# When the parts of a transposed chunk are made: moved delays in the feed-forward rounds of a two-layer decoder trunk

## The chip, the cores and the metric

The kernel runs on one core of a Trainium2 chip. The metric is the device time of one execution in microseconds (us); lower is better. Before the change the median of three runs is 2461.22 us (2460.16 to 2461.9).

## What is computed

Two decoder layers act on x, 256 positions by 2048 features in float32. Cut to what matters here:

```
for l in range(2):
    h = rms_norm(x, mix_norm[l])
    q, k, v, uv, gate_logits = split(h @ w_in[l])
    branch_a = sliding_window_attention(rope(norm(q)), rope(norm(k)), v, sinks[l]) @ w_attn_branch[l]
    branch_b = chunked_sgu(gelu(uv), w_spatial[l], b_spatial[l], ...) @ w_sgu_branch[l]
    g = sigmoid(gate_logits)
    x = x + (g[:2048] * branch_a + g[2048:] * branch_b) @ w_out[l]
    h2 = rms_norm(x, ffn_norm[l])
    x = x + (silu(h2 @ w_gate[l]) * (h2 @ w_up[l])) @ w_down[l]      # 5632 hidden features
```

In `chunked_sgu` each group of 128 features is mixed over positions by the lower triangle of a 128 by 128 matrix of `w_spatial`; the kernel needs these matrices transposed.

## The kernel before, in words

**Products.** All weights pass once through the core, in tiles of 256 rows by 512 columns (`raw`, 512 KB each). A float32 product is made of three products of parts: ScalarE rounds a weight tile to its high part (`whi`, L244), VectorE subtracts to get the low part (`wlo`, L245), and TensorE (PE) does high by high, low by high and high by low (L340, L341). The other operand, the activations, is held transposed and split in the same way: `uh` and `ul`. A list `entries`, written out before the kernel's first instruction, holds the order of all weight tiles. `step` (L343) handles one entry: it asks for weight loads up to 7 entries ahead on SyncE's queue (SP), for parts up to 4 entries ahead, and issues the entry's matmuls: twelve (both halves of 128 positions) for most entries, six for the entries of the next paragraph.

**Fewer products.** Where two products share an operand (gate and up, or two column chunks), one or two blocks of 512 rows are done with seven products of sub-blocks in place of eight, the way of Winograd. These entries are P1 to P7. P5, P6 and P7 need sums of activations, `sums`, with their own parts `sh` and `sl`, and four of the entries need differences of weight tiles (`raw<-raw,raw`, L229, on VectorE). Between P5 and P6 ScalarE takes the product in PSUM away (`kept`, L363) and copies one bank into the other (L364); P6 adds to a bank that L364 reads.

**Ticks.** `tick` (L265) comes after every twelve matmuls. `after(n, fn)` puts work on the list for the n-th tick from now. The instructions of such work stand on VectorE behind the newest weight-part instruction that has been issued there, so about three entries ahead of PE. PE's own order is as written; on the other engines the order comes from a scheduler that goes by the order of issue and by what it expects to be ready.

**Feed-forward.** The 11 chunks of 512 hidden features are done in ROUNDS of 4, 4 and 3 chunks (f0 to f1). For every chunk `hidden` (L976) makes gate and up, puts silu(gate) times up into `hid` (L981, L985) and calls `transposed` (L421). After the chunks of a round follow the products with `w_down` for these rows (`hid` plans), whose first head entries (P1, P5, P6, P2, P7, P4) are placed between the last entries of the last chunk. In rounds 1 and 2 the first three chunks use two blocks of the P kind each (`two`).

**Transposing a chunk.** `turn` (L403) transposes 32 by 32 blocks on VectorE (`box`, L410), half at the call and half one tick later, and then issues 16 DMAs of 32 KB (`tt<-box`, L416) that gather the blocks: all on the given queue, or with `queue=None` alternately on SP's and on GpSimd's (POOL). For most chunks the parts `uh`, `ul` are made 6 and 7 ticks after the call (`parts`, L435 on ScalarE and L436 on VectorE), shifted by `late`. Chunk 0 of a round, the Winograd one, runs down six steps at the ticks of a tuple such as WINO_HID: two of `scaled` (L480, ScalarE: `flat<-tt`), `whole` (L484 `uh`, L485 `ul`), two of `sums` (L499, two VectorE instructions each), and `finished` (L484 `sh`, L485 `sl`). Chunk 2 of the last round goes through PE transposes instead (L453).

In `hidden` before, the call comes 2 ticks after the chunk (1 for the fourth chunk, 3 for the last chunk of the last round), the queue is POOL's, except for the fourth chunk, which uses both.

**Spatial matrices.** `fetch_large` (L663) loads the matrices 21 and 25 ticks after a layer's start (SP, with the triangle cut on POOL, L615) and at tick 40 calls `spatial` (L648): PE turns eight of them into two PSUM buffers `pw` (L653), VectorE copies each out (L654 `wsT<-pw`). These buffers come from a pool of two, `ps_tr`, which the attention's transposed weights `ppt` (L783) use as well.

Of the kernel before, what the change touches and what calls it, by code (L numbers as in the profile page):

```python
# [33 lines left out]
WINO = 0  # L34
# [1 line left out]
WINO_IN = 6, 7, 8, 12, 13, 14  # L36
WINO_FIRST = 6, 7, 8, 9, 10, 11
WINO_MIX = 6, 7, 9, 10, 11, 13
WINO_HID = 7, 8, 17, 18, 19, 20
W_SPLIT = 4  # L40
W_TWO = 24
W_SUM = 6
# [16 lines left out]
def hybrid_trunk(ctx: ExitStack, tc: tile.TileContext, x, mix_norm, w_in, q_norm, k_norm, sinks,  # L59
                 sgu_ln_g, sgu_ln_b, w_spatial, b_spatial, w_attn_branch, w_sgu_branch, w_out,  # L60
                 ffn_norm, w_gate, w_up, w_down, cosine, sine, out):
    nc = tc.nc
# [19 lines left out]
    def slot(shape, dt=F32, name="s"):  # L82
        return big.tile(shape, dt, tag="s4", name=nm(name))
# [178 lines left out]
    def after(n, fn):  # L262
        steps.append((slot_no[0] + n, fn))

    def tick():  # L265
        slot_no[0] += 1
        due = [s for s in steps if s[0] <= slot_no[0]]
        steps[:] = [s for s in steps if s[0] > slot_no[0]]
        for _, fn in sorted(due, key=lambda s: s[0]):
            with tc.issue_after(stream.last.ins):  # L270
                fn()
# [116 lines left out]
    def product(key):  # L388

        p = run(key)  # L390
        while p.left:
            step()
        return p.acc["a"]

    def product_pair(key, on_a, on_b):


        p = run(key)
        p.calls = (on_a, on_b)
        while p.left:  # L400
            step()
# [179 lines left out]
    def mix_cols(l):  # L581
        return vcols[:, l * 16:(l + 1) * 16]

    def ffn_cols(l):
        return vcols[:, NB + l * 16:NB + (l + 1) * 16]
# [72 lines left out]
    def prepare(l):  # L658
        layer[l] = pl = Layer(l)
        after(5, lambda: pl.tables(0))  # L660
        after(6, lambda: pl.tables(1))

    def fetch_large(pl):  # L663
        for n, i in ((13, 2), (17, 3), (21, 0), (25, 1)):
            after(n, lambda i=i: pl.fetch(i))
        after(40, pl.spatial)

    class Attention:

# [210 lines left out]
    def residual(key, nxt=None, scale=1.0, store=False):  # L880

        def chunk(j, sums):
            for t in range(NT):
                n = 2 if store and j == NCH - 1 else 1
                w = CW // n
                for i in range(n):
                    sl = slice(j * CW + i * w, j * CW + (i + 1) * w)
                    nc.vector.scalar_tensor_tensor(out=xs[:, t, sl], in0=sums[t][:, i * w:(i + 1) * w], scalar=scale,  # L888
                                                   in1=xs[:, t, sl], op0=ALU.mult, op1=ALU.add)
                    if store:  # L890
                        eng = nc.sync if i == 0 else nc.scalar
                        eng.dma_start(out[0, t * P:(t + 1) * P, sl], xs[:, t, sl])
            if nxt is not None:
                last = j == NCH - 1 and not nxt.soon
                after(1 if last else 2, lambda: nxt.unit(j, j > 0 and nxt.soon, queue=None if last or j == WINO and not nxt.soon else nc.gpsimd,
                                                         late=-2 if last else 0))
                after(3, lambda: nxt.squares(j))
                if j == NCH - 1:
                    after(4, lambda: nxt.finish())
                    if not nxt.soon:  # L900
                        after(W_TWO, lambda: nxt.unit(WINO + 1, again=True))

        for j in range(0, NCH, 2):
            product_pair(key, lambda sums: chunk(j, sums), lambda sums: chunk(j + 1, sums))
        return nxt
# [4 lines left out]
    for l in range(DEPTH):  # L910

        gates = {}
        att, spa = Attention(layer[l]), Spatial(layer[l], norm)
        units_at["att", l], units_at["sgu", l] = att.attT, spa.sguT
        fetch_large(layer[l])

        def taken(kind, c):

            def by(ps):
                if kind in ("v", "u"):  # L920
                    (spa.v if kind == "v" else spa.u)(c, ps)
                    return
                dst = slot([P, NT, CW], name=kind)
                for t in range(NT):
                    nc.scalar.activation(dst[:, t, :], ps[t], AF.Tanh if kind == "gate" else AF.Copy,
                                         scale=(norm.rh if kind == "gate" else norm.r)[t])
                if kind == "gate":
                    gates[c] = dst
                else:
                    att.keys(dst) if kind == "kv" else att.queries(c, dst)  # L930
            return by

        def projected(*chunks):
            if len(chunks) == 2:
                product_pair(("in", l), taken(*chunks[0]), taken(*chunks[1]))
            else:
                taken(*chunks[0])(product(("in", l)))
                tick()

        for chunks in FIRST_PART[l]:  # L940
            projected(*chunks)


        for j in range(NCH):
            ps = product(("att", l))
            ga = gates[j]
            for t in range(NT):
                nc.vector.scalar_tensor_tensor(out=ga[:, t, :], in0=ga[:, t, :], scalar=1.0, in1=ps[t],
                                               op0=ALU.add, op1=ALU.mult)
            tick()  # L950
        mT = units_at["mix", l] = [None] * NCH
        nxt = Norm(ffn_cols(l))
        units_at["ffn", l] = nxt.units
        for j in range(NCH):
            if j == 1:
                projected(("gate", 5), ("gate", 6))
            if j == 3:
                projected(("gate", 7))
            ps = product(("sgu", l))
            ga, gb = gates[j], gates[NCH + j]  # L960
            for t in range(NT):
                nc.vector.scalar_tensor_tensor(out=gb[:, t, :], in0=gb[:, t, :], scalar=1.0, in1=ps[t],
                                               op0=ALU.add, op1=ALU.mult)
                nc.vector.tensor_tensor(out=ga[:, t, :], in0=ga[:, t, :], in1=gb[:, t, :], op=ALU.add)
            after(2 + 2 * (j == NCH - 1), lambda j=j, ga=ga: transposed(mT, j, ga, on_pe=j == NCH - 1,
                                                                   wino=WINO_MIX if j == WINO else None,
                                                                   late=3 if j == NCH - 2 else 0))
            tick()

        norm = residual(("mix", l), nxt, scale=0.5)  # L970


        if l + 1 < DEPTH:
            after(28, lambda: prepare(l + 1))

        def hidden(hT, c):  # L976
            hid = slot([P, NT, CW], name="hid")

            def on_gate(g):
                for t in range(NT):  # L980
                    nc.scalar.activation(hid[:, t, :], g[t], AF.Silu, scale=norm.r[t])  # L981

            def on_up(up):
                for t in range(NT):
                    nc.vector.scalar_tensor_tensor(out=hid[:, t, :], in0=up[t], scalar=norm.r[t], in1=hid[:, t, :],  # L985
                                                   op0=ALU.mult, op1=ALU.mult)
                pe, soon = c == len(hT) - 1 == 2, c == 3
                after(3 if pe else 1 if soon else 2,
                      lambda: transposed(hT, c, hid, on_pe=pe, wino=WINO_HID if c == WINO else None,
                                         queue=None if soon else nc.gpsimd, late=-2 if soon else 0))  # L990

            product_pair(("ffn", l), on_gate, on_up)

        for r, (f0, f1) in enumerate(ROUNDS):
            hT = units_at["hid", l, r] = [None] * (f1 - f0)
            for f in range(f0, f1):
                hidden(hT, f - f0)
            if f1 < NF:
                residual(("hid", l, r))
            elif l + 1 < DEPTH:  # L1000
                norm = Norm(mix_cols(l + 1), True)
                units_at["in", l + 1] = norm.units
                residual(("hid", l, r), norm)
            else:
                residual(("hid", l, r), store=True)
# [37 lines left out]
```

## Time and profile before

| | |
|---|---|
| median of three runs | 2461.22 us |
| the profiled execution | 2457.45 us |
| its span, first to last instruction | 2455.7 us |
| PE busy | 2438.1 us, 99% |
| VectorE (DVE) busy | 1999.5 us, 81% |
| ScalarE (ACT) busy | 1472.5 us, 60% |
| GpSimd (POOL) busy | 315.6 us, 13% |
| mean granted TensorE clock | 0.999 |

The profile names engines PE, DVE, ACT, POOL and SP; PEld is PE's weight load, SPq the queue of SyncE. A row such as `wlo<-raw,whi` names what is written and read; L245 is the line of the kernel. In the timeline the first number of a row is its start in us from the span's start, the second its length, `x2` means that two such instructions are merged, and `[1.58 <-DVE sl L485]` says that the engine stood idle for 1.58 us before it until that instruction ended. Matmuls overlap: one that takes 0.39 us in its row lets the next start earlier, so starts are compared with starts. In the waits the columns are the total in us, the times, and the longest.

### The profile page before, as it was taken

Reading aid. Unit: us, or ns where it says so; the run is one execution under the profiler, and the core shown is the slowest. Engines: PE = TensorE matmul, PEld = TensorE weight load, DVE = VectorE, ACT = ScalarE, POOL = GpSimd, SP = SyncE. Lnnn points to the kernel's source line nnn. Section 1 sums busy time; section 2 is a strip of 40 time slices with the busy share of each in tenths; the row PEclk is TensorE's granted clock in tenths of the full one; section 3 lists DMA queues with packets and bytes.
Section 4 is the critical chain, followed back from the end, with each engine's and each line's share of the span. In section 5 each row is a group of like instructions: output and inputs, shape, how many; then the busy total and the mean of one; then the engine's idle time right before and its main releaser. Section 6 shows DMA issues by size and latency. Waiting matters only on the chain.

```text
span 2455.7 us, 31363 instructions
## 1 busy us (share of the span) xinstructions
PE 2438.1 (99%) x10968; PEld 2012.6 (82%) x10968; DVE 1999.5 (81%) x2320; ACT 1472.5 (60%) x1842; POOL 315.6 (13%) x592
## 2 busy tenths in 40 slices
PE   9999999999999999999999999999999999999999
PEld 7888888888888888887887888888888888888877
DVE  6798676797978997899877986768878789978996
ACT  5567544576655665566655665545666556655664
POOL 3100002132210111001101000021322101110110
PEclk9999999999999999999999999999999999999999
DMA  9555657576667657665747446675767675667654
GB/s 299 196 187 163 212 198 220 186 236 210 220 217 233 210 176 231 230 203 170 229 155 257 152 157 223 202 215 177 246 202 236 204 245 189 200 209 241 203 179 139
DMA packets 280782, 506.74 MB, mean 206 GB/s; under 512 B 28272, under 2 KB 40144, under 8 KB 280624
## 3 DMA queue, kind: packets, MB, share of 16 engines
q1 hardware_dynamic: 262544, 486.35, 61.0%
q0 software_dynamic: 17760, 18.12, 2.8%
q8 instruction: 86, 1.41, 0.2%
q14 instruction: 72, 0.59, 0.1%
q10 hardware_dynamic: 320, 0.27, 0.0%
HBM read 475.27 MB, written 2.10 MB: 194 GB/s over the span
## 4 chain that ended last, share of the span: by engine, by line
PE 90%; DVE 3%; DMA 3%; SPq 1%; issue 1%; ACT 1%; DVEq 0%; ACTq 0%
PE acc L340 59%; PE acc L341 29%; DMA raw<-in_w_in_dram 2%; DVE wlo L245 2%; SPq L416 1%; ACT whi L244 1%; PE po L793 1%; PE psc L754 0%; PE ppt L783 0%; DVE raw L229 0%; PE psg L871 0%; PE pt L453 0%; DMA raw<-in_w_up_dram 0%; DMA raw<-in_w_down_dram 0%; DVE box L410 0%
## 5 line engine op out<-in xcount | busy, mean ns | idle before, releaser
L244 ACT ACTIVATE whi<-raw 128x1024 fp32r<-128x1024 f32 (+1 forms) x1074 | 1132.0, 1059 | 883.0 <-PE acc L341 623.4
L245 DVE TENSOR_TENSOR wlo<-raw,whi 128x1024 fp32r<-128x1024 f32 (+1 forms) x1075 | 1301.3, 1219 | 399.0 <-ACT whi L244 386.7
L340 PE MATMUL acc<-whi,uh 128*128 128x512 f32 x2994 | 1170.3, 391 | 1.2 <-ACT uh L439 1.2
L340 PE MATMUL acc<-wlo,uh 128*128 128x512 f32 x2994 | 1167.1, 390 | 3.0 <-DVE wlo L245 2.9
L341 PE MATMUL acc<-whi,ul 128*128 128x512 f32 x2994 | 1166.4, 390 | 0.0
L340 PEld LDWEIGHTS acc<-wlo,uh 128*128 128x128 f32 x2994 | 562.6, 188 | 123.2 <-DVE wlo L245 6.0
L340 PEld LDWEIGHTS acc<-whi,uh 128*128 128x128 f32 x2994 | 562.6, 188 | 117.7 <-ACT uh L439 1.4
L341 PEld LDWEIGHTS acc<-whi,ul 128*128 128x128 f32 x2994 | 562.3, 188 | 117.8 <-DVE ul L444 0.5
L416 POOL DMA_DIRECT2D tt<-box x544 | 266.5, 497 | 1697.0 <-ACT whi L244 695.5
L229 DVE TENSOR_TENSOR raw<-raw,raw 128x1024 f32<-128x1024 f32 x236 | 287.8, 1219 | 1.6 <-DMA raw<-in_w_up_dram 0.8
L341 PE MATMUL acc<-whi,sl 128*128 128x512 f32 x472 | 184.0, 390 | 3.2 <-DVE sl L485 3.2
L340 PE MATMUL acc<-whi,sh 128*128 128x512 f32 x472 | 184.8, 392 | 1.7 <-ACT acc L364 1.7
L340 PE MATMUL acc<-wlo,sh 128*128 128x512 f32 x472 | 184.2, 390 | 0.0
L341 PEld LDWEIGHTS acc<-whi,sl 128*128 128x128 f32 x472 | 88.6, 188 | 22.5 <-DVE sl L485 4.0
L340 PEld LDWEIGHTS acc<-whi,sh 128*128 128x128 f32 x472 | 88.6, 188 | 20.9 <-ACT acc L364 2.1
L340 PEld LDWEIGHTS acc<-wlo,sh 128*128 128x128 f32 x472 | 88.7, 188 | 18.0
L366 DVE TENSOR_TENSOR kept<-acc,kept 128x512 f32<-128x512 f32 x94 | 64.3, 684 | 10.1 <-PE acc L341 10.1
L369 ACT ACTIVATE acc<-kept 128x512 f32<-128x512 f32 x94 | 54.9, 586 | 4.3 <-DVE kept L366 4.2
L888 DVE SCALAR_TENSOR_TENSOR xs<-acc,xs 128x512 f32<-128x512 f32 (+1 forms) x66 | 42.0, 668 | 8.4 <-PE acc L341 8.1
L436 DVE TENSOR_TENSOR ul<-tt,uh 128x512 fp32r<-128x512 f32 x52 | 34.0, 684 | 2.9 <-ACT uh L435 2.9
L435 ACT ACTIVATE uh<-tt 128x512 fp32r<-128x512 f32 x52 | 29.8, 618 | 9.4 <-DMA tt<-box 9.4
L312 POOL TENSOR_TENSOR rv<-ve,neg_half 128x4 f32<-128x4 f32 x8 | 11.9, 1486 | 172.9 <-DVE ve L839 159.5
(137 smaller groups left out, 874.8 us busy)
## 6 DMA issues: line engine op xcount, KB each, us to landing
raw<-in_w_in_dram SPq DMA_DIRECT2D x239, 512.0 KB, 4.7
raw<-in_w_gate_dram SPq DMA_DIRECT2D x176, 512.0 KB, 4.4
raw<-in_w_up_dram SPq DMA_DIRECT2D x176, 512.0 KB, 4.9
raw<-in_w_down_dram SPq DMA_DIRECT2D x176, 512.0 KB, 5.0
raw<-in_w_out_dram SPq DMA_DIRECT2D x64, 512.0 KB, 5.0
tt<-box POOLq DMA_DIRECT2D x544, 32.0 KB, 4.2
raw<-in_w_attn_branch_dram SPq DMA_DIRECT2D x32, 512.0 KB, 5.6
raw<-in_w_sgu_branch_dram SPq DMA_DIRECT2D x32, 512.0 KB, 4.4
```

The source lines that it names most:

```text
L229: self.last = nc.vector.tensor_tensor(out=self.raws[d], in0=self.raws[x], in1=self.raws[y], op=ALU.subtract)
L244: self.high = nc.scalar.activation(hi[:, i, :], raw[:, i, :], AF.Copy)
L245: self.last = nc.vector.tensor_tensor(out=lo[:, i, :], in0=raw[:, i, :], in1=hi[:, i, :].bitcast(F32), op=ALU.subtract)
L340: nc.tensor.matmul(ps, a, part[:, kk, :], start=first and kk + n == 0, stop=False, skip_group_check=True)
L341: nc.tensor.matmul(ps, b, hi[:, kk, :], start=False, stop=kk == 1, skip_group_check=True)
L366: nc.vector.tensor_tensor(out=p.kept[:, int(tag == "P7"), :], in0=a[1], in1=p.kept[:, 1, :], op=ALU.add)
L369: nc.scalar.activation(ps, p.kept[:, t, :], AF.Copy)
L416: q.dma_start(dst[j * B:(j + 1) * B, i], box[i * B:(i + 1) * B, j])
L435: nc.scalar.activation(h, s_, AF.Copy)
L436: nc.vector.tensor_tensor(out=l, in0=s_, in1=h.bitcast(F32), op=ALU.subtract)
L793: nc.tensor.matmul(po[:, h, :], pT[kb][:, h, :], self.kv[:, kb, KVW + g * HD:KVW + (g + 1) * HD], start=kb == 0, stop=kb == t)
L888: nc.vector.scalar_tensor_tensor(out=xs[:, t, sl], in0=sums[t][:, i * w:(i + 1) * w], scalar=scale, in1=xs[:, t, sl], op0=ALU.mult, op1=AL ...
```

## The change

It moves work to other ticks and one gather to other queues; no instruction that computes is added or taken away.

```diff
-WINO_HID = 7, 8, 17, 18, 19, 20
+WINO_HID = 11, 12, 17, 18, 19, 20
+WINO_END = 9, 10, 12, 13, 14, 15
...
         for n, i in ((13, 2), (17, 3), (21, 0), (25, 1)):
             after(n, lambda i=i: pl.fetch(i))
-        after(40, pl.spatial)
+        after(34, pl.spatial)
...
-                pe, soon = c == len(hT) - 1 == 2, c == 3
+                pe, soon = c == len(hT) - 1 == 2, c == 3 or c == 1 and len(hT) == 3
                 after(3 if pe else 1 if soon else 2,
-                      lambda: transposed(hT, c, hid, on_pe=pe, wino=WINO_HID if c == WINO else None,
-                                         queue=None if soon else nc.gpsimd, late=-2 if soon else 0))
+                      lambda: transposed(hT, c, hid, on_pe=pe, wino=None if c != WINO else WINO_HID if len(hT) == 4 else WINO_END,
+                                         queue=None if soon else nc.gpsimd, late=-2 if c == 3 else 4 if c == 1 and len(hT) == 4 else 2 if c == 2 else 0))
```

In words, for both layers:

- In the last round (3 chunks) chunk 0 makes `scaled` 2 ticks later, and `whole`, `sums` and `finished` 5 ticks sooner.
- In the last round chunk 1 is transposed 1 tick sooner, its 16 gathers go 8 to SP and 8 to POOL, and its parts come 1 tick sooner.
- In the rounds of 4 chunks, `scaled` of chunk 0 comes 4 ticks later, the parts of chunk 1 come 4 ticks later, and those of chunk 2 come 2 ticks later.
- The spatial matrices are turned at tick 34 of a layer, not 40.

## The prediction

> **What bounds the kernel now.** I read the page first, then the waits of PE, then the timeline around each wait.
>
> ```profile
> span 2455.7 us, 31363 instructions
> PE 2438.1 (99%) x10968; PEld 2012.6 (82%) x10968; DVE 1999.5 (81%) x2320; ACT 1472.5 (60%) x1842; POOL 315.6 (13%) x592
> ...
> PE acc L341 <- DVE sl L485: 3.2, 2, 1.6
> PE acc L340 <- DVE wlo L245: 2.9, 5, 0.8
> PE ppt L783 <- DVE wsT L654: 2.4, 1, 2.4
> PE acc L340 <- ACT acc L364: 1.7, 1, 1.7
> ```
>
> PE bounds it, and nearly all of its time is work that the change leaves alone: 2455.7 − 2438.1 leaves 17.6 us of idle time, the first and last moments included. The four waits named are 10.2 us of that. A change that only moves other engines' work can win those waits and what hangs on them, some 10 us or 0.4%, and no more. So each wait is looked at by itself.
>
> The pitch of a full matmul is needed throughout:
>
> ```profile
> 2359.83 0.39 PE L340 MATMUL acc<-wlo,uh 128*128 128x512 f32 x1
> ...
> 2362.55 0.39 PE L340 MATMUL acc<-wlo,uh 128*128 128x512 f32 x1
> ```
>
> Twelve matmuls, one tick, lie between these two: 2.72 us, 0.227 each.
>
> **Part 1: the last round's first sums.** In the second layer:
>
> ```profile
> 2374.34 0.39 PE L341 MATMUL acc<-whi,ul 128*128 128x512 f32 x1
> ...
> 2377.03 0.50 PE L341 MATMUL acc<-whi,sl 128*128 128x512 f32 x1 [1.58 <-DVE sl L485]
> 2377.37 0.39 PE L340 MATMUL acc<-whi,sh 128*128 128x512 f32 x1
> ```
> ```profile
> 2370.21 0.42 DVE L499 TENSOR_TENSOR sums<-flat 128x256 f32<-128x256 f32 x1
> ...
> 2375.76 1.22 DVE L485 TENSOR_TENSOR sl<-sums,sh 128x1024 fp32r<-128x1024 f32 x1
> ```
>
> The reader sees PE at P5 waiting for `sl`, which VectorE ends at 2376.98. From 2374.34 to 2377.37 four pitches (0.91) took 3.03 us: 2.12 lost. The waits say twice, so each layer has it. WINO_END moves `finished` from 20 to 15: 5 × 2.72 = 13.6 us sooner, so `sl` would start about 2362.2, and even some us late it is there before PE asks at 2375.06. The gather that feeds it ends much earlier than `scaled`, which itself goes two ticks later. I take the whole: **−4.2** for both layers (bounds: 0 if the queues carry it late all the same, −4.2).
>
> **Part 2: the second chunk.** After P5, the second layer alone shows another gap:
>
> ```profile
> 2383.29 0.39 PE L341 MATMUL acc<-whi,ul 128*128 128x512 f32 x1
> ...
> 2385.69 0.40 PE L340 MATMUL acc<-wlo,sh 128*128 128x512 f32 x1
> ```
> ```profile
> 2381.04 1.06 ACT L244 ACTIVATE whi<-raw 128x1024 fp32r<-128x1024 f32 x1 [1.67 <-PE acc L341]
> 2382.01 1.13 ACT L435 ACTIVATE uh<-tt 128x512 fp32r<-128x512 f32 x2
> ...
> 2384.73 0.58 ACT L364 ACTIVATE acc<-acc 128x512 f32<-128x512 f32 x1
> ```
>
> Two pitches (0.45) took 2.40: 1.95 lost. P6 waits for L364 (the waits' last row), which stands in ScalarE's queue behind L435, the second chunk's parts, and behind a `whi` that itself waits for PE. P5's product was complete long before: its sixth matmul starts three pitches after 2377.03. One tick sooner (2.7 us), the parts go ahead of this, and `sh` (1.06) leaves the stretch as well. I take **−1.95**; bounds 0 and −1.95. The gather itself is 16 issues in two batches of 3.91 us on POOL; half of them go to SP, past weight loads:
>
> ```profile
> 716.91 6.07 SPq L416 DMA_DIRECT2D tt<-box  x8
> ...
> 1326.13 10.66 SPq L416 DMA_DIRECT2D tt<-box  x16
> ```
>
> The first row is the fourth chunk of round 0, which already uses both queues: SP is held for 6 us, and no PE wait stands near. In the last round ScalarE's `whi` waits for PE, as the row at 2381.04 says, and not for its load, so I cost the hold at 0; the price without that cover is the second rival's.
>
> **Part 3: VectorE where the sums land.** Here the change pays. Around 2350 VectorE has no gap:
>
> ```profile
> 2350.00:2363.00 13.00, 13.00 (x59) 10.75 (x58) 13.00 (x15) 7.26 (x9) 0.00 (x0) 1.00 0.78 259
> ...
> 2358.72 1.22 DVE L245 TENSOR_TENSOR wlo<-raw,whi 128x1024 fp32r<-128x1024 f32 x1
> 2359.85 0.70 DVE L410 STREAM_TRANSPOSE box<-hid 128x512 f32<-128x512 f32 x1
> 2360.48 2.32 DVE L245 TENSOR_TENSOR wlo<-raw,whi 128x1024 fp32r<-128x1024 f32 x2
> ```
>
> In the first row the third busy time, VectorE's, is 13.00 of 13.00. The `wlo` of 2358.72 ends at 2359.94 and PE reads it at 2362.55 (above): 2.61 us of slack. By the ticks `whole`, four `sums` and one `box` are now issued ahead of it. Queued, an instruction holds VectorE about 0.08 less than its row's length (0.70 for `box`, but the next starts 0.63 later), so they are 1.14 (`ul`, as long as `sl`) + 4 × 0.34 + 0.62 = 3.12 us. The `wlo` is 0.51 late. The next one, from 2360.48, also has `sl` and the second `box` ahead: 1.76 more; it ends about 2365.9, its PE time moves from 2365.27, one tick after 2362.55, to 2365.78: 0.14 late. Each pause costs its first matmul 0.1 (2377.03 to 2377.37 is 0.34). Together 0.85. In the first layer the slack is smaller:
>
> ```profile
> 1137.11 1.22 DVE L245 TENSOR_TENSOR wlo<-raw,whi 128x1024 fp32r<-128x1024 f32 x1
> ...
> 1140.71 0.39 PE L340 MATMUL acc<-wlo,uh 128*128 128x512 f32 x1
> ```
>
> 1140.71 − 1138.33 = 2.38, so 0.23 more: 1.1. I take **+2.0**, from the order of issue and these slacks. Bounds: 0, if the scheduler lets the urgent `wlo` pass; +9.8, if all the moved work, 2 × 1.14 + 4 × 0.34 + 2 × 0.62 = 4.9 us a layer, meets no slack at all. Nothing else new waits on VectorE; ScalarE, with 7.26 busy of 13.00 in that row, has room for `uh` and `sh`.
>
> **Part 4: spatial matrices.**
>
> ```profile
> 1340.91 1.03 PE L653 MATMUL pw<-ident,wsraw 128*128 128x128 f32 x8
> 1341.88 0.72 PE L754 MATMUL psc<-kT,qT 64*128 64x128 f32 x8
> 1345.03 0.66 PE L783 MATMUL ppt<-ident,pr 128*128 128x128 f32 x4 [2.43 <-DVE wsT L654]
> 1345.44 0.48 PE L340 MATMUL acc<-whi,uh 128*128 128x512 f32 x1
> ...
> 1349.40 0.40 PE L340 MATMUL acc<-wlo,uh 128*128 128x512 f32 x1
> ```
> ```profile
> 1341.80 2.57 DVE L245 TENSOR_TENSOR wlo<-raw,whi 128x1024 fp32r<-128x1024 f32 x2 [5.75 <-ACT whi L244]
> 1344.29 1.28 DVE L654 COPY wsT<-pw 128x512 f32<-128x512 f32 x2
> ...
> 1346.10:1349.10 3.00, 3.00 (x9) 2.33 (x8) 3.00 (x5) 1.26 (x3) 0.00 (x0) 0.50 0.69 247
> ```
>
> In the second layer, tick 40 is also a tick of attention. `pw` takes both `ps_tr` buffers, the copies stand behind two late `wlo`, and `ppt` waits for a buffer. Six ticks earlier are 72 matmuls (16.3 us), one set of scores (0.65) and the pause below (1.1): about 1322.8, where PE has a hole:
>
> ```profile
> 1322.58 0.47 PE L340 MATMUL acc<-whi,uh 128*128 128x512 f32 x1
> ...
> 1324.15 0.40 PE L341 MATMUL acc<-whi,ul 128*128 128x512 f32 x1
> ```
>
> Two pitches took 1.57, so 1.1 idle; the eight transposes (0.97, by the next start) fit in. There the copies (1.28) fall behind parts issued three entries ahead of PE, and well before the 5.75 us in which VectorE idles. At the old place only `psc` (0.7) and `ppt` (0.41) stay: PE is at its product at 1342.0, but the first `wlo` ends at 1343.0, so the second matmul starts there, which is like a start at 1342.8. 1345.44 − 1342.8 = 2.6 won. Next late is then the load behind SP's 10.66 us gather, which is that 1343.0.
>
> There is more. After the gap matmuls run at half speed: the last row's clock column says 0.50, and the ten steps from 1345.44 to 1349.40 took 3.96 in place of 2.27, 1.7 lost. With 0.2 for the pause left, the second layer wins 4.1. [...]
>
> The first layer:
>
> ```profile
> 122.95 0.50 PE L340 MATMUL acc<-wlo,uh 128*128 128x512 f32 x1 [0.57 <-DVE wlo L245]
> ...
> 125.58 1.03 PE L653 MATMUL pw<-ident,wsraw 128*128 128x128 f32 x8
> ```
>
> Here `pw` comes after a pause of 0.57 for a late weight, and the first matmul then costs 0.1 more. With 0.97 us of transposes done before it, PE arrives later and the pause goes: −0.7. The copies then stand on VectorE near 110 us, behind parts made ahead of PE, and are waited for by nobody before the mixing. Together **−4.8**. Bounds: −0.7, if in the second layer the copies or the weights hold PE as long as now; −5.0, if the pause left there goes too.
>
> **Part 5: the rounds of four.** In round 1 the second chunk's parts (L436) go through VectorE shortly before a low part is late:
>
> ```profile
> 919.43 0.39 PE L341 MATMUL acc<-whi,ul 128*128 128x512 f32 x1
> 919.88 0.50 PE L340 MATMUL acc<-wlo,uh 128*128 128x512 f32 x1
> ```
>
> 0.45 − 0.23 = 0.2 lost; four ticks later (10.9 us) the parts are past it. For both layers **−0.4**. The other moves there meet no wait of PE: 0, bounds −0.2 and +0.4 by the same row.
>
> **The sum.** −4.2 − 1.95 + 2.0 − 4.8 − 0.4 = −9.4 us (−11.4 without the toll of part 3). Against the profiled execution, 2457.45 (the span and 1.75 around it), that is 2448.1. The median of the runs is 3.8 above the profiled execution; I carry the difference over: 2461.2 − 9.4 = **2451.8 us**. A measurement of this kernel can tell about 0.2%, 4.9 us, from no change.
>
> **Rivals.**
> 1. *VectorE's toll is larger.* If all 4.9 us lie ahead of the `wlo` read at 2362.55 and its like, the toll is 4.9 − 2.61 + 4.9 − 2.38 + 0.2 = 5.0, and the time 2454.8; with no slack, 9.8, and 2459.6. For: no idle time in 13 us. Against: the slacks, and parts issued in turn. Chance 0.16.
> 2. *SP's half of the gather holds up weight loads; slower.* Place: SP's queue in the last round, where the gather first waits for the second `box`. A hold of 10.66 us cost PE at most 0.7 by the rows at 1326 and 1342; a longer one costs one for one. From a hold of 10.66 − 0.7 + 9.4/2 = 14.7 us in each layer on, the kernel is slower. Eight issues take 6; the other 9 would be spent waiting for a `box` late by that much. With 17.2 us per layer: 2466.3. Against: fully busy VectorE was late by about 3 us in part 3. Chance 0.07.
> 3. *The half clock is not in every run.* If the timed runs of before mostly miss it, 1.7 of part 4 isn't there to win: 2453.5. [...] Against: the profiled execution has it and is no slower than the timed ones. [...] Chance 0.12.
> 4. *It doesn't do what it says in the last round.* The order off PE is the scheduler's; L364 was late in one layer and not in the other with the same ticks. If parts 1 and 2 stay as they are and part 3 costs nothing: −5.2, 2456.0. Chance 0.15.
>
> My forecast keeps 0.5, with a range of its own of 2449.5 to 2454 (no toll, or twice the toll). The range for 8 in 10 reaches over rivals 1, 3 and 4: 2449.5 to 2459.5. Faster by over 0.2% means below 2456.3: the forecast, rival 3, and half or more of 1 and 4, 0.78. Same 0.15, slower 0.07.
>
> **What would show it.** Right: no PE wait for `sl`, `wsT` or L364; a `pw` at about 1322 with no 0.50 clock near 1346; one short wait of PE for `wlo` in each last round, near 1141 and 2363. Wrong: `sl` still ending within 2 us of P5; PE waits over 2 us for `wlo` there; ScalarE waiting for `raw` of `w_down`; or a new wait where nothing was moved.

## The result, and the profile after

| | before | after |
|---|---|---|
| median of five runs each | 2460.76 us (2460.16 to 2461.9) | 2449.74 us (2449.56 to 2451.44) |
| the profiled execution | 2457.45 us | 2449.56 us |
| its span | 2455.7 us | 2447.8 us |

The change is faster: ratio 0.9957, 95% interval 0.9942 to 0.9971. The forecast was 2451.8 us in a range of 2449.5 to 2459.5. The timed runs moved by 11.0 us, the profiled executions by only 7.9; where the other 3.1 may come from is taken up below. The change adds a line above the rest, so L340 of before is L341 of after, L364 is L365, and so on.

From the page of after:

```profile
span 2447.8 us, 31373 instructions
...
PE 2436.2 (100%) x10968; PEld 2012.2 (82%) x10968; DVE 1999.0 (82%) x2320; ACT 1470.0 (60%) x1842; POOL 310.6 (13%) x576
```

The waits of PE in after (total, times, longest):

```profile
PE acc L341 <- DVE wlo L246: 2.8, 7, 0.6
PE acc L341 <- DVE kept L367: 1.4, 2, 1.0
PE acc L341 <- ACT uh L440: 1.3, 1, 1.3
PE pwarm L292 <- DVE warm L287: 1.1, 1, 1.1
```

The three waits that the forecast set out to win (`sl`, `wsT`, the copy of one bank into the other) are gone from the list, 7.3 us in all. Those for `wlo` are about as large as before, and one for `kept` (L367) now stands second.

Where P5 gave way to P6 in the second layer, PE's timeline in after shows no gap of two microseconds any more:

```profile
2371.01 0.39 PE L342 MATMUL acc<-whi,sl 128*128 128x512 f32 x1
...
2377.13 0.39 PE L342 MATMUL acc<-whi,ul 128*128 128x512 f32 x1
2377.39 0.50 PE L341 MATMUL acc<-whi,sh 128*128 128x512 f32 x1
```

VectorE's and ScalarE's timelines say why. `sl` ends at 2365.26, 5.7 us before PE reads it, and the second chunk's parts leave ScalarE before the copy (L365), which ends at 2377.33, just when P6 asks:

```profile
2364.03 1.23 DVE L486 TENSOR_TENSOR sl<-sums,sh 128x1024 fp32r<-128x1024 f32 x1
```
```profile
2373.13 1.14 ACT L436 ACTIVATE uh<-tt 128x512 fp32r<-128x512 f32 x2
...
2376.73 0.60 ACT L365 ACTIVATE acc<-acc 128x512 f32<-128x512 f32 x1
```

At the spatial place `pw` stands where it was expected, and `ppt` follows `psc` without a wait:

```profile
1321.24 1.03 PE L654 MATMUL pw<-ident,wsraw 128*128 128x128 f32 x8
...
1340.09 0.66 PE L784 MATMUL ppt<-ident,pr 128*128 128x128 f32 x4
1340.50 0.48 PE L341 MATMUL acc<-whi,uh 128*128 128x512 f32 x1
1340.82 0.39 PE L341 MATMUL acc<-wlo,uh 128*128 128x512 f32 x1
```
```profile
1340.05 2.57 DVE L246 TENSOR_TENSOR wlo<-raw,whi 128x1024 fp32r<-128x1024 f32 x2 [4.63 <-ACT whi L245]
```

The last row, from VectorE's timeline, is the pair of `wlo` that stood at 1341.80 in before. Its first half takes over 1.2 us, so it is not done when PE's matmul on `wlo` starts at 1340.82: PE does not wait for this pair there.

New in after are two pauses of PE 25 to 30 us further on, and two smaller ones like them in the first layer, at 156.78 and 159.11:

```profile
1366.80 0.50 PE L341 MATMUL acc<-wlo,uh 128*128 128x512 f32 x1 [0.51 <-DVE wlo L246]
1370.55 0.50 PE L341 MATMUL acc<-wlo,sh 128*128 128x512 f32 x1 [0.95 <-DVE kept L367]
```

PE's order is the same in both kernels, so the traces can be laid over each other, product matmul by product matmul, and each change of the difference between the two starts put down to its place:

| term | forecast | trace of after less that of before |
|---|---|---|
| 1, first sums | −4.2 | −2.13 and −2.13, +0.17 at P6 behind the first |
| 2, second chunk | −1.95 | −1.81 |
| 3, toll on VectorE in the last rounds | +2.0 | +0.22 in layer 1; +0.69 (at 2331 to 2340) and +0.22 (at 2356) in layer 2 |
| 4, spatial matrices | −4.8 | −0.35 in layer 1; −5.2 in layer 2, 1.59 of it the half clock |
| new pauses in attention | none | +1.3 in layer 1, +1.9 in layer 2 |
| 5, rounds of four | −0.4 | −0.39 and −0.39 |
| all product matmuls, first to last | −9.4 | −8.1 |

The rows leave out shifts of 0.2 us and less elsewhere. One execution of each kernel is compared, and executions differ: in e2 to e6 below, where the first layer's matrices stay at tick 40, the place of row 4 in layer 1 shows −0.35 to −0.46 as well, so this −0.35 is not shown to come from the move. In the other kernels that move them (e1, e7 to e12) it is −0.80 to −1.22, which makes the move worth some 0.4 to 0.8 us there and nothing in the execution of after.

Two questions remain: what gave some 3.2 us back in attention, and whether the parts do alone what they do together.

### The profile page after: what moved, and what is told of

It reads as the page before. It is cut to its first block, busy times and chain, and to the rows that moved or that the text cites. A ratio compares the mean times of both kernels' runs of the same rounds, so it can differ in the third digit from the quotient of the medians.

```text
span 2447.8 us, 31373 instructions
## 1 busy us (share of the span) xinstructions
PE 2436.2 (100%) x10968; PEld 2012.2 (82%) x10968; DVE 1999.0 (82%) x2320; ACT 1470.0 (60%) x1842; POOL 310.6 (13%) x576
## 4 chain that ended last, share of the span: by engine, by line
PE 93%; DVE 3%; DMA 1%; issue 1%; ACT 1%; SPq 0%; POOL 0%; DVEq 0%; ACTq 0%; POOLq 0%
PE acc L341 61%; PE acc L342 30%; DVE wlo L246 1%; DMA raw<-in_w_in_dram 1%; PE po L794 1%; DVE raw L230 0%; SPq L417 0%; PE psc L755 0%; PE ppt L784 0%; PE pt L454 0%; ACT whi L245 0%; PE psg L872 0%; DMA raw<-in_w_up_dram 0%; DVE pr L759 0%; DVE mx L763 0%
## 5 line engine op out<-in xcount | busy, mean ns | idle before, releaser
L341 PE MATMUL acc<-whi,uh 128*128 128x512 f32 x2994 | 1171.3, 391 | 1.3 <-ACT uh L440 1.3
L341 PE MATMUL acc<-wlo,uh 128*128 128x512 f32 x2994 | 1168.2, 390 | 2.8 <-DVE wlo L246 2.8
L341 PEld LDWEIGHTS acc<-wlo,uh 128*128 128x128 f32 x2994 | 562.5, 188 | 123.3 <-DVE wlo L246 7.9
L341 PEld LDWEIGHTS acc<-whi,uh 128*128 128x128 f32 x2994 | 562.5, 188 | 117.4 <-ACT uh L440 1.5
L417 POOL DMA_DIRECT2D tt<-box x528 | 258.6, 497 | 1698.4 <-ACT whi L245 568.1
L341 PE MATMUL acc<-wlo,sh 128*128 128x512 f32 x472 | 184.6, 391 | 1.4 <-DVE kept L367 1.4
L341 PE MATMUL acc<-whi,sh 128*128 128x512 f32 x472 | 185.0, 392 | 0.0
L341 PEld LDWEIGHTS acc<-wlo,sh 128*128 128x128 f32 x472 | 88.7, 188 | 20.1 <-DVE kept L367 2.2
L341 PEld LDWEIGHTS acc<-whi,sh 128*128 128x128 f32 x472 | 88.7, 188 | 18.6 <-ACT acc L365 0.6
L367 DVE TENSOR_TENSOR kept<-acc,kept 128x512 f32<-128x512 f32 x94 | 64.4, 685 | 8.7 <-PE acc L342 8.7
```

The source lines that it names most:

```text
L341: nc.tensor.matmul(ps, a, part[:, kk, :], start=first and kk + n == 0, stop=False, skip_group_check=True)
L367: nc.vector.tensor_tensor(out=p.kept[:, int(tag == "P7"), :], in0=a[1], in1=p.kept[:, 1, :], op=ALU.add)
L417: q.dma_start(dst[j * B:(j + 1) * B, i], box[i * B:(i + 1) * B, j])
```

## The experiments

Theory: each edit removes the wait that the forecast names, the edits add up, and what is given back is VectorE's load. The rivals are written into each expectation. Differences "by place" are found as in the table above, against before. Ratios are to before, measured beside each kernel.

### The parts alone

**e1: the spatial matrices alone.** Before, with

```diff
-        after(40, pl.spatial)
+        after(34, pl.spatial)
```

> Part 4 alone: the spatial matrices at tick 34, all else as before. Theory G (given back): the wait for wsT at 1345 and the half clock after it go (5.2 us in the profile of the changed kernel), but VectorE then has no lead in the attention stretch that follows, and new pauses of PE near 156-160 (1.3 us) and 1366-1371 (1.8 us) come with it; profiled span 2.4 us shorter, by 1.5 to 3.5. Theory I (independent): the new pauses belong to other parts of the change, or to chance in the scheduler's order; then the span is 4.5 to 5.5 us shorter. In both, no wait for wsT and no 0.5 clock near 1346.

Measured: 2455.61 us, ratio 0.9986 (0.9977 to 0.9995), span 2453.4. By place the wins are those of after (layer 2: +0.80, −1.02, −3.38 and −1.59), and the pauses come too: +1.45 in all at 156 to 159, +2.46 at 1369 to 1373. PE's timeline of e1:

```profile
1369.23 0.50 PE L340 MATMUL acc<-wlo,uh 128*128 128x512 f32 x1 [1.12 <-DVE wlo L245]
...
1372.98 0.50 PE L340 MATMUL acc<-wlo,sh 128*128 128x512 f32 x1 [0.95 <-DVE kept L366]
```

So the pauses belong to this edit and to no other: Theory G.

**e2: everything but the spatial matrices.** After, with

```diff
-        after(34, pl.spatial)
+        after(40, pl.spatial)
```

> The change without part 4. Theory G: no pauses of PE over 0.5 us near 156-160 and 1366-1371; the wait for wsT near 1345 and the half clock are back; profiled span 5.5 us shorter than before (2 x 2.1 + 1.8 + 0.8 - 1.1). Theory I: the pauses are there all the same, and the span is 2.5 us shorter. For the timed runs: if the difference between 11.0 (timed) and 7.9 us (profiled) is a matter of half clock windows that the wsT wait brings, the timed gain here stays near 5.5; if it is something else, it is near 8.

Measured: 2452.9 us, ratio 0.9972 (0.9962 to 0.9982), span 2452.1. No such pause in attention; the wait for `wsT` is back (3.0 us), and the mean granted clock is 0.998, against 1.000 in after. The span is only 3.6 us shorter than before's, not 5.5: by place its matmuls near the start lie some 2.5 us behind. The timed gain, 6.6, lies between the 5.5 and the 8 of the expectation and decides nothing. In medians e1 gives −3.8 and e2 −6.6, in sum −10.4, against −11.0 for after: these two halves add up.

**e3: the sums alone.** Before, with WINO_END for chunk 0 of the last round and nothing else:

```diff
-wino=WINO_HID if c == WINO else None,
+wino=None if c != WINO else WINO_HID if len(hT) == 4 else WINO_END,
```

Here WINO_HID keeps its old values.

> Part 1 alone: WINO_END for chunk 0 of the last round. Forecast by the prediction: PE's wait for sl goes in both layers (-4.2), the toll on VectorE comes (+0.2 in the first layer, +0.9 in the second, as the changed kernel's profile has it, against 2.0 on record), and the wait for L364 stays in the second layer (1.8 to 1.95): span 3.1 us shorter. Rival: the toll comes from chunk 1's earlier blocks and not from the sums; then no pause for wlo and 4.2 us shorter.

Measured: 2464.17 us, ratio 1.0019 (1.0011 to 1.0028), span 2461.9: slower than before, where 3.1 us less was expected. The wait for `sl` goes in both layers, −2.13 each. But ScalarE's timeline in the first layer reads:

```profile
1158.62 1.06 ACT L245 ACTIVATE whi<-raw 128x1024 fp32r<-128x1024 f32 x1 [1.54 <-issue]
1161.34 1.06 ACT L245 ACTIVATE whi<-raw 128x1024 fp32r<-128x1024 f32 x1 [1.66 <-PE acc L342]
1162.30 1.13 ACT L436 ACTIVATE uh<-tt 128x512 fp32r<-128x512 f32 x2
1163.34 0.57 ACT L364 ACTIVATE kept<-acc 128x512 f32<-128x512 f32 x1
1163.95 0.58 ACT L365 ACTIVATE acc<-acc 128x512 f32<-128x512 f32 x1
```

and PE's:

```profile
1164.58 0.50 PE L341 MATMUL acc<-whi,sh 128*128 128x512 f32 x1 [3.33 <-ACT acc L365]
```

The sums on VectorE push the second chunk's `box` back. The first POOL gather starts at 1145.82, against 1142.45 in before; PE itself is 1.2 to 1.6 later there, so about 2 us later for PE. PE, on the other hand, comes 2.1 us sooner. The copy that P6 needs stands on ScalarE behind the parts, and these behind a `whi` that waits for PE. P6 is 3.79 and 1.75 late by place, and each time matmuls at half clock follow, 0.43 us apart in place of 0.23 (1.45 and 1.52 us lost by place).

**e4: the second chunk alone.** Before, with

```diff
-                pe, soon = c == len(hT) - 1 == 2, c == 3
+                pe, soon = c == len(hT) - 1 == 2, c == 3 or c == 1 and len(hT) == 3
...
-queue=None if soon else nc.gpsimd, late=-2 if soon else 0))
+queue=None if soon else nc.gpsimd, late=-2 if c == 3 else 0))
```

> Part 2 alone: chunk 1 of the last round one tick sooner, gathered on both queues. By the prediction the wait for L364 goes (-1.9) and the waits for sl stay (3.2 us in all): span 1.9 us shorter. Rival: L364 is late because of sh and the first sums in ScalarE's queue, which part 1 moves; then the wait for L364 stays and the span is within 0.5 us of before.

Measured: 2457.47 us, ratio 0.9993 (0.9984 to 1.0001), span 2456.9. By place the copy's wait goes in layer 2, −1.89; `sl` is waited for as before. In medians e3 and e4 come to +4.7 − 2.0 = +2.7, though e4's interval reaches 1. Together, in e2, which has the rounds of four besides (0 to 0.8 us, e5), they give −6.6. So they do not add: 8 to 9 us hang on their being done at once.

**e5: the rounds of four alone.** Before, with

```diff
-wino=WINO_HID if c == WINO else None,
+wino=None if c != WINO else WINO_HID if len(hT) == 4 else WINO_OLD,
...
-late=-2 if soon else 0))
+late=-2 if c == 3 else 4 if c == 1 and len(hT) == 4 else 2 if c == 2 else 0))
```

Here WINO_HID is 11, 12, 17 to 20 as in after, and WINO_OLD the tuple of before.

> The two edits of the rounds of four chunks alone (the WINO_HID sums four ticks later, the second and third chunks' parts later), the last rounds and the spatial matrices as before. Theory of the prediction: 0.4 us less (0.2 per layer); the trace of after, laid over that of before, showed 0.46 and 0.38, so the median should lie 0.4 to 0.9 us under the kernel before and no wait of PE that the kernel before has should go. Rival: the two edits only pay because the other parts move VectorE's and ScalarE's work, and alone they do nothing, within 0.2 us.

Measured: 2459.32 us, ratio 0.9998 (0.9989 to 1.0007). By place −0.39 and −0.35, as expected, but the profiled execution has a mean granted clock of 0.998, against 0.999 in before, and a span of 2458.0, 2.3 us longer; the timed runs do not resolve it.

### One queue or one tick

**e8: the gather on POOL alone, one tick sooner; e9: both queues, at the old tick.** After, with

```diff
 # e8
-queue=None if soon else nc.gpsimd
+queue=None if c == 3 else nc.gpsimd
...
 # e9
-                pe, soon = c == len(hT) - 1 == 2, c == 3 or c == 1 and len(hT) == 3
+                pe, soon = c == len(hT) - 1 == 2, c == 3
-queue=None if soon else nc.gpsimd
+queue=None if soon or c == 1 and len(hT) == 3 else nc.gpsimd
```

> After, but the last round's second chunk is gathered from POOL's queue alone, still one tick sooner than in before. Theory of the prediction (the tick is what removes the wait for L365, the second queue only makes the landing sooner): the gather lands some us later than in after, and if that is before ScalarE takes the parts the time is after's within 0.3 us. Rival (both queues are needed): L365's wait comes back in one layer or both, 1.8 to 3.8 us longer.

> After, but the last round's second chunk is transposed and gathered at the old tick (2), though from both queues. Theory Q (one queue alone issues its sixteen parts in two bursts of 3.9 us, 5 us apart, so that the parts stand in ScalarE's queue behind two casts that wait for PE; a second queue halves that): the gather lands one tick (2.7 us) later than in after and the parts are late by between 0 and 2.7 us, so L365's wait comes back in part: 0 to 2.7 us per layer over after, far less than the 4.5 per layer of one queue at the new tick. Theory T (the tick counts, the queues do not): as with one queue, 9 us over after.

e8: 2463.95 us, ratio 1.002 (1.001 to 1.0029), span 2460.6. e9: 2450.59 us, ratio 0.9961 (0.9948 to 0.9975), span 2447.7, that of after. POOL's queue in e8:

```profile
1145.01 3.91 POOL L417 DMA_DIRECT2D tt<-box  x8 [33.90 <-DVE sums L500]
1150.02 3.91 POOL L417 DMA_DIRECT2D tt<-box  x8 [1.10 <-DMA tt<-box]
```

and POOL's and SP's queues in after, where both halves run at once:

```profile
1144.89 3.90 POOL L417 DMA_DIRECT2D tt<-box  x8 [33.03 <-DVE sums L500]
```
```profile
1144.48 6.59 SPq L417 DMA_DIRECT2D tt<-box  x8
```

ScalarE's timeline, first in e8, then in after:

```profile
1157.81 1.06 ACT L245 ACTIVATE whi<-raw 128x1024 fp32r<-128x1024 f32 x1 [1.66 <-PE acc L342]
1160.53 1.06 ACT L245 ACTIVATE whi<-raw 128x1024 fp32r<-128x1024 f32 x1 [1.66 <-PE acc L342]
1161.49 1.13 ACT L436 ACTIVATE uh<-tt 128x512 fp32r<-128x512 f32 x2
...
1164.30 0.58 ACT L365 ACTIVATE acc<-acc 128x512 f32<-128x512 f32 x1
```
```profile
1154.02 2.02 ACT L245 ACTIVATE whi<-raw 128x1024 fp32r<-128x1024 f32 x2 [1.75 <-DVE raw L230]
1155.94 1.14 ACT L436 ACTIVATE uh<-tt 128x512 fp32r<-128x512 f32 x2
...
1159.55 0.60 ACT L365 ACTIVATE acc<-acc 128x512 f32<-128x512 f32 x1
```

The reader sees that the second batch of eight starts 5.0 us after the first, waiting for transfers of the first to land, and that the parts then go behind two more `whi` that PE has to release. It is their place in ScalarE's order that holds them, and not the landing itself: in e8 the last transfer of this gather lands at 1157.41 by the trace, and the parts start 4.1 us later, behind the second `whi`; in after it lands at 1153.53 and they start 2.4 us later. That the scheduler chose this order because it reckoned with a later gather fits what it goes by, but no run shows its reasons. PE waits 4.5 us at each P6. The row for e8 in its waits of PE:

```profile
PE acc L341 <- ACT acc L365: 9.0, 2, 4.5
```

The span is 12.8 us longer than after's: these 9.0, and part of the rest at half clock. Behind the first P6 ten matmul steps, 1165.52 to 1169.79, took 4.27 us in place of 2.27, and the mean granted clock is 0.998, against 1.000 in after.

The theory of the prediction (the tick does it) falls with e8, and its rival holds with more than its 1.8 to 3.8 us. The queues carry part 2 and the tick does not: with both queues POOL's gather starts at 1145.03 at the old tick (e9) and at 1144.89 at the new one, and in both the profile ends POOL's idle time with the same VectorE instruction (`sums`, L500). Theory Q holds in what it says of the queues and in its time, at the lower end of its range; its landing 2.7 us later at the old tick did not come (0.1 earlier in layer 1, 0.6 later in layer 2). Theory T wanted 9 us over after, and the medians differ by 0.9. On one queue the sixteen issues took 8.9 us in e8 (2 × 3.91 and the 1.10 between); on two they took 3.90 on POOL and 6.59 on SP in after, at the same time.

### The pauses in attention

**e6: the spatial matrices sooner in layer 2 only.** After, with

```diff
-        after(34, pl.spatial)
+        after(40 if pl.l == 0 else 34, pl.spatial)
```

> After, but with the spatial matrices issued at 40 (as before) in layer 1 and at 34 in layer 2 alone. Theory G (the sooner matrices put VectorE's attention work back to back, so that PE then waits for wlo and kept): the pauses of 0.6 and 0.9 us near 156.8 and 160.4 go, the move of 0.35 gained near 107 to 127 is given back, and the profile is about 1.0 us shorter than that of after. Rival (those pauses come from another part of the change, or from the execution): they stay, and the time is 0.3 us longer than after's.

Measured: 2450.99 us, ratio 0.9965 (0.9953 to 0.9978), span 2446.8: 1.0 under the span of after, as expected, with no pause left near 157 to 160. That the sum fits is in part chance: by place the pauses give 1.3, the 0.35 is not given back, and layer 2's pauses are 0.7 larger than in after. In the medians the difference does not show (spread 2448.17 to 2451.22). PE comes to this place only 0.3 us sooner than in e6; what differs is VectorE's order, first in after and then in e6:

```profile
156.63 1.21 DVE L763 TENSOR_REDUCE mx<-pr 128x4 f32<-128x1024 f32 x1
...
157.83 2.36 DVE L246 TENSOR_TENSOR wlo<-raw,whi 128x1024 fp32r<-128x1024 f32 x2
```
```profile
156.13 1.22 DVE L246 TENSOR_TENSOR wlo<-raw,whi 128x1024 fp32r<-128x1024 f32 x1
157.27 1.22 DVE L763 TENSOR_REDUCE mx<-pr 128x4 f32<-128x1024 f32 x1
```

In after the softmax's maximum `mx` goes ahead of the `wlo` that PE waits for at 159.11; in e6 it goes behind. VectorE has no idle time in either stretch.

**e10: the centring of v 8 ticks later.** After, with

```diff
-                after(4 + 3 * t, lambda t=t: self.center(c, t))
+                after(12 + 3 * t, lambda t=t: self.center(c, t))
```

> After, but each centring of v in the spatial attention is issued 8 ticks later, so that it lies behind the stretch where PE pauses in after (156 to 161 and 1366 to 1371). Theory G (VectorE is back to back there, and wlo and kept come late for it): those pauses shrink, 1.3 us in layer 1 and 1.8 in layer 2, so up to 3.1 us less than after, less what the centrings collide with where they now lie. Rival (the pauses come from ScalarE or from a buffer's release, not from VectorE's load): no change within 0.3 us, or a new wait for the centred v, and slower.

Measured: 2447.71 us, ratio 0.9953 (0.994 to 0.9966), span 2444.8: 3.0 under that of after. The ratios of the two overlap, so the timed runs do not resolve it, and the traces decide. Twenty microseconds around the pauses, by engine (PE, PEld, DVE, ACT, POOL; granted clock), at about the same work in before, in after and in e10:

```profile
1361.60:1381.60 20.00, 20.00 (x105) 16.14 (x104) 20.00 (x40) 14.55 (x26) 1.92 (x1) 1.00 0.49 164
```

```profile
1352.00:1372.00 20.00, 18.54 (x89) 14.61 (x88) 19.10 (x41) 11.12 (x20) 3.14 (x2) 1.00 0.38 109
```
```profile
1351.80:1371.80 20.00, 20.00 (x98) 16.31 (x97) 17.91 (x23) 12.21 (x23) 0.00 (x0) 1.00 0.49 145
```

In before VectorE has no gap there either (20.00), but PE comes later and finds its parts ready. In after PE is sooner and waits; in e10 VectorE goes from 41 instructions to 23 and PE from 18.54 to 20.00. Both pauses of each layer are gone. But the centring of the second half of v now meets attention 55 to 60 us later, and PE's timeline in e10 has two new ones, +1.1 and +0.7 by place:

```profile
213.61 0.50 PE L341 MATMUL acc<-wlo,uh 128*128 128x512 f32 x1 [0.83 <-DVE kept L367]
```
```profile
1427.08 0.50 PE L341 MATMUL acc<-wlo,uh 128*128 128x512 f32 x1 [0.42 <-DVE kept L367]
```

By place the old pauses give 3.5 us, the wait for `att` near 1404 another 0.6, and the new ones take 1.8. The rest of the 3.0 lies at places that differ from execution to execution.

**e12: only the first half later** (and the sums of e7, below). After, with `WINO_END = 9, 10, 14, 15, 16, 17` and

```diff
-                after(4 + 3 * t, lambda t=t: self.center(c, t))
+                after((4 if c else 12) + 3 * t, lambda t=t: self.center(c, t))
```

> As the kernel with both the centring and the sums later, but only the first half of v is centred 8 ticks later, the second half at its old place. Theory G (each pause of PE is where VectorE's queue is back to back, so work is to be put where the queue has room): the pauses of 0.85 near 213 and of 0.57 near 1427, which came with the later centring of the second half, go, and the pauses at 156 to 161 and 1366 to 1371 do not come back, so 1.4 us less than with both halves later (a span near 2442.7). Rival (the later centring only pushes the same lateness about): the pauses move to another place, and the span stays within 0.4 us of 2444.1 or grows.

Measured: 2445.56 us (2444.47 to 2447.83), ratio 0.9943 (0.993 to 0.9957), span 2442.6, the shortest of all; 2442.7 was expected. The pauses near 213 and 1427 go, those near 157 and 1366 stay away, and the wait for `kept` is gone from the list:

```profile
PE acc L341 <- DVE wlo L246: 1.5, 3, 0.7
PE pwarm L292 <- DVE warm L287: 1.1, 1, 1.1
PE acc L341 <- ACT uh L440: 1.1, 1, 1.1
```

The theory is shown by the traces: the pauses are VectorE's load at that place, and moving other work of VectorE away removes them. The ratios of e12 and of after still overlap.

### The toll in the last rounds

**e7: the sums two ticks later; e11: the same, with the centring of e10.** After (e11: e10), with

```diff
-WINO_END = 9, 10, 12, 13, 14, 15
+WINO_END = 9, 10, 14, 15, 16, 17
```

> After, with the last round's sums two ticks later (finished at 17, not 15). Theory of the prediction (the sums, put among the first chunks' products, make wlo late on VectorE; the toll is 0.2 in layer 1 and 0.9 in layer 2 by the laid-over traces): sl is still there before PE asks for it, since it was 2 us late at 20 and moves 8 us sooner, and a part of the 1.1 us of toll goes, so the time is 0 to 1 us under after's. Rival 1 (the toll is not the sums' but that of the second chunk's box and scaled): no change. Rival 2 (sl comes late again, behind the box transposes): 2 us per layer come back, and slower than after by up to 4.

> After, with both the centring of v 8 ticks later and the last round's sums two ticks later. If the two give-backs are VectorE's load at two different places they add: 3.0 us for the centring (its own profile against after's) and 0 to 1 for the sums, so 2444 to 2447.5 and the shortest of all. If the sums' move is worth nothing or harms, the time is that of the later centring alone, 2447.7, or that much more.

e7: 2449.42 us, ratio 0.9955 (0.994 to 0.9971), span 2449.3. e11: 2447.22 us, ratio 0.9949 (0.9936 to 0.9961), span 2444.1. The +0.22 of layer 1 and the +0.22 of layer 2 are gone from both. The +0.69 is not: it is 1.18 in e7 and 0.42 in e11. VectorE's timeline in after shows what it is:

```profile
2326.12 1.23 DVE L246 TENSOR_TENSOR wlo<-raw,whi 128x1024 fp32r<-128x1024 f32 x1 [0.70 <-ACT whi L245]
2328.46 1.22 DVE L230 TENSOR_TENSOR raw<-raw,raw 128x1024 f32<-128x1024 f32 x1 [1.12 <-DMA raw<-in_w_up_dram]
```

The first of the sums (L500) comes at 2353.37, 25 us later. What is late at 2328 is a load of `in_w_up`, which lands while chunk 0's gather runs (issued on POOL from 2317.95 to 2328.30). In before the same instruction waits 0.21. In the other kernels it waits 0.11 to 0.51 where the last round's second chunk is gathered by one queue (e1, e3, e5, e8), 0.59 to 1.64 where it is gathered by two (e2, e6, e7, e9 to e12), and 0 in e4, which has two. That gather is issued only some 35 us after this wait, one execution of each was profiled, and nothing tried here tells a cause from chance: it stays open. So a toll of the sums exists: at these two places the kernels with the sums as in after (e2, e3, e6, e8 to e10) lose between 0 and 0.23 us a layer, and those with the sums later or as before lose none. By the timed runs e7's move is worth nothing that they resolve.

## Why the prediction was right, and where it was not

**Part 1 was right in its size and wrong in standing alone.** 2.13 in each layer, for −4.2. But the step "even some us late it is there" looked only at `sl`. Of the second chunk's `box` behind the new sums it asked nothing, and e3 shows that this turns 4.3 us won into a slower kernel. The sum added parts 1 and 2 as if each could be had without the other.

**Part 2 was right in its size, and its step "one tick sooner (2.7 us), the parts go ahead of this" failed.** In layer 1 the tick brought the gather's start 0.1 us (e9). The second queue, costed only for what it might hold up, does the work (e8).

**Part 3: the term of +2.0 measured 0.4 for the sums.** The forecast put `whole` and all four sums ahead of the urgent `wlo`, by the order of issue. VectorE's order in after mixes them, and `sl` goes behind the urgent parts, the lower bound's "if the scheduler lets the urgent `wlo` pass". Layer 2's 0.91 looks like the forecast 0.85, but 0.69 of it lies at the late load of `in_w_up`. A number that fits is no proof of its mechanism.

**Part 4: −4.8 measured −5.5 at its own place, and −2.3 with what it gave back.** The step "the copies are waited for by nobody" holds. In layer 2 the wait was mis-sized: 3.4 us and not 2.6. The forecast held PE until the `wlo` of 1341.80 ends, and PE's product there does not read it, as the rows of after show; 1345.44 − 1342.0 was the whole gap. In layer 1 the −0.7 is not seen in after, and is some 0.4 to 0.8 in the other kernels with the move. The part's failure is in what it did not ask. In layer 2, with `ppt` no longer late, PE reaches the products behind it some 5 us sooner, and VectorE, which has the softmax, the centring of v and the weight parts there, is then 1.9 us late. In layer 1 PE is hardly sooner, and with VectorE's changed order 1.3 us go. "Where a stall goes, say what is late next" was answered for the next matmul, and not for the 30 us behind it. e10 and e12 show that VectorE's load is what is late; that PE's coming sooner sets it off in layer 2, and a new order in layer 1, is read from the traces and was not tried alone.

**Part 5** was right in its place, and its term too small by half: 0.8 measured for 0.4 in the profile, 0.2 for the late matmul, 0.1 for the next and some hundredths around them in each layer. The timed runs do not resolve it alone.

**The sum.** −9.4 in the profile was −8.1. The forecast then carried over the 3.8 us by which the median of before lay above its profiled execution. In after the median lies only 0.2 above, which made the timed gain larger. So 2451.8 came within 2.1 us of 2449.74 partly by luck: 1.5 us too much gain in the sum (−9.4 for the −7.9 between the profiled executions), 3.6 too little in what the timed runs add.

**The rivals.** 1 did not come in the last round; its mechanism did, in attention. 2 did not come: SP's half took 6.59 us and ScalarE waited for no `w_down`. Nothing of 4 either. 3 came with the other sign. The half clock is indeed not the same in every execution (before's profiled one is at 0.999, its timed ones at 0.997 to 1.000), but the timed runs of before seem to meet more of it than its profiled execution, not less. Each timed run beside the experiments has a mean granted clock. Among the 69 such runs of before the mean time is 2456.64 at 1.000 (2 runs), 2458.71 at 0.999 (20), 2459.90 at 0.998 (42) and 2461.73 at 0.997 (5), about 1.7 us for each 0.001. After's five runs are at 0.999 to 1.000. A half clock of 3.41 us takes 3.41 × 0.5 / 2455 = 0.0007 off that mean, so most runs of before hold two to four of them, and those of after none to two. At about 1.5 us each (1.45 to 1.59 by place in e3 and before) that is of the size of the missing 3.1. But this is an estimate from clocks of three decimals, since the timed runs have no trace, and the five runs of before in the result have no clock on record. Beside the experiments the median of before lay at 2459.2 to 2459.7, so 1.0 to 1.5 us of the 3.1 may as well be the spread of five runs. It stays open.

## What to carry to other kernels

When a stall is won, lay the new starts over the old ones for the next tens of microseconds and ask each engine's queue there, since PE comes sooner and whoever had slack has less. Edits that meet in one queue are not terms of a sum: run each alone, as one that pays with its neighbour can lose without it. Look in an engine's timeline, ScalarE's here, for a copy that PE needs standing behind work that itself waits for PE: in e8, where two more `whi` stood ahead of it, PE waited 4.5 us each time.

## What the runs showed of the hardware

**Behind some waits of PE 3.41 us went at half the clock, behind others none.** Two stretches of e4, behind the waits for `sl` (first layer) and for `wsT`, each in two pieces (PE busy, granted clock):

```profile
1153.63:1157.04 3.41, 1.83 (x7) 1.00 0.71 168
1157.04:1160.45 3.41, 3.41 (x9) 0.50 0.41 147
1344.77:1348.18 3.41, 0.39 (x7) 1.00 1.05 386
1348.18:1351.59 3.41, 3.41 (x11) 0.50 0.83 306
```

and two of before, at the waits for `wsT` and for `sl` (second layer):

```profile
1342.46:1345.88 3.42, 0.99 (x10) 1.00 1.05 392
1345.88:1349.29 3.41, 3.41 (x10) 0.50 0.67 241
2373.27:2376.68 3.41, 2.18 (x9) 1.00 0.90 252
2376.68:2380.09 3.41, 3.06 (x13) 1.00 0.40 145
```

In three of these pairs a piece in which PE is busy for 0.39 to 1.83 us is followed by one at 0.50. In the fourth, whose wait lies in both pieces, the clock stays at 1.00, and so it does behind before's wait for `sl` in the first layer, 1.58 us idle (1.00 from 1156 to 1162). So here a stall's price was its length plus, at times, about 1.5 us: 1.59 by place behind `wsT` in before, 1.45 and 1.52 behind the two late P6 of e3. Why one wait was followed by it and another was not is not shown.
